# Router fed with centred rows, the last two tiles routed one by one in a written order, and gathered rows in other memory

## The chip, the cores and the metric

The kernel runs on one core of a Trainium2 chip. The number that counts is the device time of one execution in microseconds (us). The engines of the core are named as the profile names them: PE (TensorE, matrix products; PEld loads its weights), DVE (VectorE), ACT (ScalarE), POOL (GpSimd) and SP (SyncE, which here only issues DMAs).

## What the program computes

One hybrid decoder layer over 2048 tokens of width 1024, in float32. Only the end of the mixer, the router and the experts matter here:

```
mix = concatenate([y_conv, y_dn]) @ w_out
x   = layer_norm(ALPHA * x + gate1 * mix, ln1_g, ln1_b)
h   = x * (1 + scale2) + shift2
group   = top 1 of softmax(h @ w_grp + b_grp)                 # 4 groups
experts = top 2 of softmax((h @ w_exp + b_exp)[group])        # 8 experts in a group
y[token] += gate * ((silu(xb @ w_gate[e]) * (xb @ w_up[e])) @ w_down[e])   # for each chosen expert e
x = layer_norm(ALPHA * x + gate2 * y, ln2_g, ln2_b)
```

The tokens' rows h are regrouped by expert: each token has two entries (token, weight) in lists of the 32 experts, and an expert's rows are fetched by its list.

## The kernel before, in words

The program has a mixer stage and an expert stage. At the end of the mixer stage the 2048 tokens are 16 tiles of 128 rows (`mix_tile`, t = 0 to 15). For each tile PE makes two halves of `mix` (n = 0, 1), each of 24 products of 128x512: 8 slices k of the contraction, and for each slice three products, because both operands are split into a high and a low part (`y_hi`, `y_lo`, `wo_hi`, `wo_lo`). DVE adds the old x to each half and sums the row (L896), ACT squares and sums (L900), DVE finds the inverse deviation by three Newton steps on 128x1 numbers (`ln_root`, L918 to L924) and makes two normalised rows from x: `h` for the router and the experts (G2, B2) and `x_t` for the residual (Ga, Ba), two DVE instructions of 128x1024 each (L903, L904). SP stores both to DRAM (`d_h2`, `d_xa`).

Router work lags behind the tiles: `mix_tile` puts functions into the list `later`, and takes one out at fixed points (`slots`) of the following tiles. `logits` turns a tile's h by eight PE transposes into PSUM (`hT`), copies them by ACT (`hTs`) and multiplies by the router's weights (`lg`, 8 products that run as 16 passes of 128x40). `route` runs for a pair of tiles (t-1, t): DVE finds group, experts and weights (L951 to L991). `rank` finds each entry's place in the experts' lists (L999 to L1022; five small PE products count the tokens ahead), and POOL writes the entries into `d_list` with indirect DMAs, two for each tile (L1025). What is left in `later` after tile 15 (its logits, and route and rank of the pair 14, 15) is done by `flush`, behind the last product.

Meanwhile the weights of experts 0 and 1 (gate and up) are loaded while tiles are left to do (`load_first`), and `split_up(0)` makes a high part (ACT, `gu_hi`) and a low part (DVE, `gu_lo`) of those of expert 0.

The expert stage (`moe`) issues in this order on SP: down weights of expert 0 (`load_down(0)`), gate and up weights of expert 2 (`load_up(2)`), down weights of expert 1, and then the first six lists of each of two blocks (`entries`, tile `idx`), which wait until all entries have landed in `d_list`. POOL then gathers the rows of expert 0 and of expert 1 (`gather`, `hr<-d_h,idx`, 512 KB each), PE turns them (`pT`), ACT and DVE split them (`xT_hi`, `xT_lo`), and the first expert's products begin (`pg`). From then on PE goes through 32 experts.

In the mixer stage a scheduler of the framework sets the order on every engine, from the order in which the code issues and from estimated costs; inside `manual_schedule` (before: `moe` on all engines, `tail` on SP) the engines named keep the order of the code. Each engine runs its instructions strictly in order, and SP's DMA issues wait on SP for what they depend on. Tiles come from pools; a tile that reuses memory waits for what last used it.

Of the kernel before, what the change touches and what calls it, by code (L numbers as in the profile page):

```python
# [10 lines left out]
F32 = mybir.dt.float32  # L11
# [9 lines left out]
P = 128  # L21
D = 1024
# [31 lines left out]
class Layer:  # L54
# [774 lines left out]
    def router_consts(self):  # L829
# [10 lines left out]
        nc.gpsimd.iota(self.iota, pattern=[[1, 32]], base=0, channel_multiplier=0, allow_small_or_imprecise_dtypes=True)  # L840
        self.tok = c.tile([P, NT, 2], I32, name="tok")
# [32 lines left out]
    def mix_tile(self, t):  # L874
        nc = self.nc
        v = nc.vector
# [3 lines left out]
        sm = lambda n, w=1: self.small.tile([P, w], F32, tag="n_" + n, bufs=2, name=n)  # L880
        st, nm, ssq = sm("st", 2), sm("nm"), sm("ssq")

        slots = ((0, 7), (1, 3)) if t % 2 else ((1, 1), (1, 5))
        for n in range(2):
            ps = self.acc("mix")
            i = 0
            for k in range(KD):
                for a, b in ((hi, 0), (hi, 1), (lo, 0)):
                    nc.tensor.matmul(ps, a[:, k, :], self.wo[n][b][:, k, :], start=i == 0, stop=i == 3 * KD - 1)  # L889
                    i += 1  # L890
                if k % 2:
                    yield
                if (n, k) in (slots if t else ((0, 3), (0, 7), (1, 3))) and self.later:
                    self.later.pop(0)()
            xs = x[:, n * 512:(n + 1) * 512]
            v.scalar_tensor_tensor(xs, xs, ALPHA, ps, op0=OP.mult, op1=OP.add, accum_out=st[:, n:n + 1])  # L896

        h = self.t4(name="h2")
        v.tensor_scalar(nm, st[:, 0:1], st[:, 1:2], -1.0 / D, op0=OP.add, op1=OP.mult)
        nc.scalar.activation(h, x, AF.Square, bias=nm, accum_out=ssq)  # L900
# [12 lines left out]
    def ln_root(self, ssq, sm):  # L913

        v = self.nc.vector
        ve, hv, rs, t = sm("ve"), sm("hv"), sm("rs"), sm("t")
        i = self.small.tile([P, 1], I32, tag="n_i", bufs=2, name="rsi")
# [4 lines left out]
        for _ in range(3):  # L922
            v.scalar_tensor_tensor(t, rs, hv, rs, op0=OP.mult, op1=OP.mult)
            v.scalar_tensor_tensor(rs, t, 1.5, rs, op0=OP.add, op1=OP.mult)  # L924
        return rs


    def logits(self, t, h):
        nc = self.nc
# [8 lines left out]
        if t % 2 == 0:  # L938
            self.pl = self.prt.tile([P, 512], F32, tag="rt", name="lg")
        o = t % 2 * 40  # L940
        for k in range(KD):
            nc.tensor.matmul(self.pl[:, o:o + 40], hT[k // 4][:, (k % 4) * P:(k % 4 + 1) * P], self.wr[:, k, :], start=k == 0, stop=k == KD - 1)

    def route(self, t):
# [4 lines left out]
        sm = self.rs_ = lambda n, s, dt=F32: self.small.tile([P] + list(s), dt, tag="r_" + n, bufs=2 if n in ("ent", "pi", "ge", "d", "ew") else 1, name=n)  # L949
# [9 lines left out]
        ex, se = sm("ex", (4,)), sm("se", (2,))  # L959
        for j in range(2):  # L960
# [5 lines left out]
        v.tensor_tensor(oh, self.iota[:, None, 0:4].to_broadcast([P, 2, 4]), gi[:, :, None].to_broadcast([P, 2, 4]), op=OP.is_equal)  # L966
        t84 = sm("t84", (2, 8, 4))
        for j in range(2):
# [5 lines left out]
        for j in range(2):  # L974
# [8 lines left out]
        for j in range(2):  # L983
# [9 lines left out]
    def rank(self, t):  # L993
        nc = self.nc
        v = nc.vector
        pl, ent, sm = self.pl, self.ent, self.rs_
# [9 lines left out]
        pr = pl[:, 128:224]  # L1006
        mm = nc.tensor.matmul
        mm(pr[:, 0:32], self.Us, ob[:, 0], start=True, stop=True)
        mm(pr[:, 32:64], self.ob, ob[:, 0], start=True, stop=False)
        mm(pr[:, 32:64], self.Us, ob[:, 1], start=False, stop=True)  # L1010
        mm(pr[:, 64:96], self.ob, ob[:, 0], start=True, stop=False)
        mm(pr[:, 64:96], self.ob, ob[:, 1], start=False, stop=True)
        rk = sm("rk", (2, 32))
        v.tensor_tensor(rk, pr[:, 0:64].rearrange("p (j c) -> p j c", j=2), self.base[:, None, :].to_broadcast([P, 2, 32]), op=OP.add)
        v.tensor_tensor(self.base, self.base, pr[:, 64:96], op=OP.add)
        for j in range(2):
# [6 lines left out]
        for j in range(2):  # L1023
# [16 lines left out]
    def moe_pools(self, st):  # L1040
        p = lambda **k: self.pool(st, **k)
# [648 lines left out]
```

## Time and profile before

| | us |
|---|---|
| median of 3 runs (lowest, highest) | 1768.59 (1767.44, 1770.77) |
| the profiled execution | 1770.56 |
| its span, first to last instruction | 1768.9 |
| mean granted PE clock, share of full | 0.956 |

| stretch of the profiled execution, us | length | PE busy | granted clock | DMA share |
|---|---|---|---|---|
| 1100 to 1166, mixer's last tiles | 66 | 65.93 | 1.00 | 0.37 |
| 1166 to 1205, between last mix product and first expert product | 39 | 7.85 | 0.52 | 0.49 |
| 1300 to 1400, experts | 100 | 94.35 | 1.00 | 0.91 |

Busy is the time in which an engine executes; idle time of an engine costs only where others wait for it. The granted clock is the share of 2.4 GHz that PE was given: 1.00 is 2.4 GHz, 0.50 is 1.2 GHz. In a row of the timeline the numbers are start and duration, then engine, source line, operation, the tile written and those read, the shape, how many instructions were merged, and in brackets how long the engine was idle ahead of it and for whom.

### The profile page before, as it was taken

The page shows a single profiled execution, that of the slowest core. Times are in us where ns is not written, and L with a number is a line of the kernel's source. Part 1 is how long each engine was busy: PE and PEld are TensorE (multiplying, and loading weights), DVE is VectorE, ACT ScalarE, POOL GpSimd, SP SyncE. Part 2 cuts the span into 40 slices and gives each one's busy share as a digit, 9 for nine tenths or more (in the row PEclk, how much of TensorE's full clock was granted, in tenths as well). Part 3 has the DMA queues.
Part 4 walks back from the last instruction along what each step waited for, and adds up shares of the span by engine and source line. Part 5 has one row for each costly group of instructions (what it writes and reads, how often), then busy time and mean ns, then how long its engine had stood idle before and what let it go on. Part 6 is the DMA issues. An engine that isn't in the chain of part 4 may idle for free. (4 is left out here: it accounts for less than half of the span.)

```text
span 1768.9 us, 25248 instructions
## 1 busy us (share of the span) xinstructions
PE 1565.4 (88%) x7784; PEld 1261.1 (71%) x7784; DVE 1254.1 (71%) x3010; ACT 775.4 (44%) x1603; POOL 534.7 (30%) x441
## 2 busy tenths in 40 slices
PE   6899999998999999999889999957999989999800
PEld 4678877776777778888678888845777778778600
DVE  6777667766877987574688887665667686876554
ACT  4433455445233336344443322226545565554452
POOL 3200111021110003022320211215556675765517
PEclk9999999999999999999999999978999999999955
DMA  9553586455764758544477854347989998998464
GB/s 282 166 184 100 167 249 192 127 136 161 219 198 144 214 163 252 141 99 118 143 241 227 256 168 144 138 160 224 298 259 290 285 316 265 294 305 240 105 221 178
DMA packets 347943, 356.79 MB, mean 202 GB/s; under 512 B 49705, under 2 KB 283778, under 8 KB 347794
## 3 DMA queue, kind: packets, MB, share of 16 engines
q1 hardware_dynamic: 330546, 316.61, 56.4%
q0 software_dynamic: 17248, 38.37, 9.2%
q8 instruction: 71, 1.16, 0.3%
q14 instruction: 78, 0.64, 0.1%
HBM read 268.83 MB, written 101.79 MB: 210 GB/s over the span
## 5 line engine op out<-in xcount | busy, mean ns | idle before, releaser
L280 PE MATMUL acc<-hhi,w_hi 128*128 128x512 f32 x896 | 365.6, 409 | 7.4 <-ACT st L444 3.2
L280 PE MATMUL acc<-hlo,w_hi 128*128 128x512 f32 x896 | 360.6, 403 | 1.7 <-DVE hlo L337 1.0
L280 PE MATMUL acc<-hhi,w_lo 128*128 128x512 f32 x896 | 361.0, 403 | 0.0
L280 PEld LDWEIGHTS acc<-hhi,w_hi 128*128 128x128 f32 x896 | 171.3, 191 | 48.6 <-ACT st L444 4.1
L280 PEld LDWEIGHTS acc<-hlo,w_hi 128*128 128x128 f32 x896 | 170.7, 191 | 40.8 <-DVE hlo L337 2.4
L280 PEld LDWEIGHTS acc<-hhi,w_lo 128*128 128x128 f32 x896 | 170.9, 191 | 39.7 <-issue 1.7
L1093 DVE TENSOR_TENSOR gu_lo<-gu_raw,gu_hi 128x1024 fp32r<-128x1024 f32 (+1 forms) x132 | 179.7, 1404 | 24.1 <-ACT gu_hi L1092 15.7
L1102 POOL TENSOR_TENSOR dn<-dn_raw,dn 128x1024 fp32r<-128x1024 f32 x64 | 168.2, 2655 | 58.4 <-ACT dn L1101 56.1
L1135 PE MATMUL pg<-gu_hi,xT_hi 128*128 128x512 f32 x376 | 150.0, 399 | 1.2 <-ACT xT_hi L1125 1.2
L1135 PE MATMUL pg<-gu_hi,xT_lo 128*128 128x512 f32 x376 | 147.5, 392 | 0.1
L1135 PE MATMUL pg<-gu_lo,xT_hi 128*128 128x512 f32 x376 | 147.3, 392 | 0.0
L1092 ACT ACTIVATE gu_hi<-gu_raw 128x1024 fp32r<-128x1024 f32 (+1 forms) x132 | 129.0, 1035 | 4.6 <-PE mix L889 2.8
L1168 PE MATMUL pd<-dn,hT_hi 128*128 128x512 f32 x376 | 120.6, 402 | 6.2 <-PEq L1211 2.5
L453 DVE SCALAR_TENSOR_TENSOR cv<-st,cw,cv 128x512 f32<-128x512 f32 x144 | 108.5, 754 | 2.1
L1182 POOL DMA_INDIRECT d_xa<-y,idx x47 | 77.1, 1640 | 105.9 <-DVE y L1176 46.3
L889 PE MATMUL mix<-wo_hi,y_hi 128*128 128x512 f32 x256 | 105.1, 411 | 0.0
L889 PE MATMUL mix<-wo_hi,y_lo 128*128 128x512 f32 x256 | 103.6, 404 | 1.2 <-DVE y_lo L871 1.2
L889 PE MATMUL mix<-wo_lo,y_hi 128*128 128x512 f32 x256 | 103.5, 404 | 0.0
L347 ACT ACTIVATE w_hi<-raw 128x1024 fp32r<-128x1024 f32 x56 | 59.6, 1065 | 93.4 <-PE acc L280 75.5
L1126 DVE TENSOR_TENSOR xT_lo<-pT,xT_hi 128x512 fp32r<-128x512 f32 x94 | 60.6, 686 | 39.1 <-ACT xT_hi L1125 35.2
L575 POOL TENSOR_SCALAR_AFFINE_SELECT gam<-gam 128x512 f32<-128x512 f32 x16 | 11.2, 701 | 252.7 <-ACT gam L574 241.7
L1168 PEld LDWEIGHTS pd<-dn,hT_hi 128*128 128x128 f32 x376 | 67.1, 188 | 27.4 <-issue 7.0
(352 smaller groups left out, 3255.1 us busy)
## 6 DMA issues: line engine op xcount, KB each, us to landing
dn_raw<-in_w_down_dram SPq DMA_DIRECT2D x32, 1024.0 KB
gu_raw<-in_w_gate_dram SPq DMA_DIRECT2D x60, 512.0 KB
gu_raw<-in_w_up_dram SPq DMA_DIRECT2D x60, 512.0 KB
raw<-in_w_in_dram SPq DMA_DIRECT2D x56, 512.0 KB
ada_w<-in_w_ada_dram SPq DMA_DIRECT2D x96, 256.0 KB
qkvT<-cv SPq DMA_DIRECT2D x48, 256.0 KB
x_t<-in_x_dram SPq DMA_DIRECT2D x16, 512.0 KB
y_raw<-yT SPq DMA_DIRECT2D x16, 512.0 KB
```

The costliest lines, as they stand in the source:

```text
L280: self.nc.tensor.matmul(ps, a[:, k, :], b[q][:, k, :], start=k + n == 0, stop=k == KD - 1 and n == 2)
L347: nc.scalar.activation(hi, raw, AF.Copy)
L453: nc.vector.scalar_tensor_tensor(y, st[:, t:t + 512], self.cw4[:, j, t:t + 1], y, op0=OP.mult, op1=OP.add)
L575: nc.gpsimd.affine_select(gam, gam, pattern=[[0, H], [1, P]], compare_op=OP.is_ge, fill=0.0, base=0, channel_multiplier=-1)
L889: nc.tensor.matmul(ps, a[:, k, :], self.wo[n][b][:, k, :], start=i == 0, stop=i == 3 * KD - 1)
L1092: nc.scalar.activation(hi[:, c], r, AF.Copy)
L1093: i = nc.vector.tensor_tensor(lo[:, c], r, hi[:, c].bitcast(F32), op=OP.subtract)
L1102: nc.gpsimd.tensor_tensor(dn[:, 1, k], r[:, k], dn[:, 0, k].bitcast(F32), op=OP.subtract)
L1126: nc.vector.tensor_tensor(lo[:, c], pT[n], hi[:, c].bitcast(F32), op=OP.subtract)
L1135: self.nc.tensor.matmul(ps, a[:, k], b[:, k], start=n == 0, stop=n == 3 * KD - 1)
L1168: self.nc.tensor.matmul(ps[n], hT[a][:, k], dn[:, b, k, c], start=i == 0, stop=i == 5)
L1182: i = self.nc.gpsimd.indirect_dma_start(out=self.d_xa, out_offset=bass.IndirectOffsetOnAxis(ap=idx[:, 0:1], axis=0), in_=y, in_offset=None ...
```

## The change

Four things change together.

- **Centred rows.** The router's products take (x - mean) * G2, without the division by the deviation and without B2. Each tile's inverse deviation stays in a tile `roots`, and `route` multiplies the logits by it (one DVE instruction for each tile in place of one for the pair). The part of B2 is put through the same transposes and products once (`router_bias`, in tile 1) and added to the router's bias. The normalised h is finished after the logits (`finish`), the residual x by `finish_x`.
- **Tiles 14 and 15 are routed one by one**, each with its own route, rank and lists.
- **Tile 15 is issued in an order by hand** (`last_tile`) on PE, ACT, DVE and SP, with the split of expert 0's weights in it. The stores of `x_t` of tiles 14 and 15 come at its end.
- **In `moe`** the first lists are read before `load_up(2)` and `load_down(1)`, not after; the pool of the gathered rows (`hrp`) is made ahead of that of the raw weights, which gives both other addresses.

```diff
 def mix_tile(self, t):
-        slots = ((0, 7), (1, 3)) if t % 2 else ((1, 1), (1, 5))
+        slots = ((0, 7), (1, 3)) if t % 2 else ((1, 1), (1, 5)) if 0 < t < NT - 2 else ((0, 3), (0, 7), (1, 3))
...
-        rs = self.ln_root(ssq, sm)
-        for o, g, b in ((h, self.G2, self.B2), (x, self.Ga, self.Ba)):
-            v.scalar_tensor_tensor(o, x, nm, g, op0=OP.add, op1=OP.mult)
-            v.scalar_tensor_tensor(o, o, rs, b, op0=OP.mult, op1=OP.add)
-        nc.sync.dma_start(self.d_h2[t * P:(t + 1) * P, :], h)
-        nc.sync.dma_start(self.d_xa[t * P:(t + 1) * P, :], x)
-        self.later.append(lambda: self.logits(t, h))
+        self.center(t, x, lo, h)
+        self.ln_root(t)
+        if t == NT - 2:
+            self.last = x, h
+            return
+        self.finish_x(t, x)
+
+        def logits():
+            self.logits(t, h)
+            self.finish(t, h)
+        self.later.append(logits)
         if t % 2:
             self.later += [lambda: self.route(t - 1), lambda: self.rank(t - 1)]
         if t == 0:
-            self.later.insert(0, lambda: None)
+            self.later.insert(0, self.router_bias)
...
+    def center(self, t, x, lo, h, parts=1):
...
+        v.tensor_scalar(nm, st[:, 0:1], st[:, 1:2], -1.0 / D, op0=OP.add, op1=OP.mult)
+        nc.scalar.activation(lo.rearrange("p k c -> p (k c)"), x, AF.Square, bias=nm, accum_out=ssq)
+        for i in range(parts):
+            c = slice(i * D // parts, (i + 1) * D // parts)
+            v.scalar_tensor_tensor(h[:, c], x[:, c], nm, self.G2[:, c], op0=OP.add, op1=OP.mult)
...
+    def last_tile(self):
...
+        mix(0, 0, 1)
+        turned = self.products_turn(h0)
+        mix(0, 1, 6)
+        self.pl = self.prt.tile([P, 512], F32, tag="rt", name="lg")
+        self.products_sum(self.pl[:, 0:40], turned)
+        mix(0, 6, KD)
+        self.finish(t - 1, h0)
+        self.route(t - 1, 1)
+        self.rank_count(t - 1, 1)
+        self.mix_sum(t, 0, ps[0], x)
+        ps.append(self.acc("mix"))
+        mix(1, 0, 6)
+        self.rank_sums(1)
+        mix(1, 6, KD)
...
+        self.rank_place(t - 1, 1)
+        self.mix_sum(t, 1, ps[1], x)
+        h = self.t4(name="h2")
+        self.center(t, x, lo, h, 2)
+        turned = self.products_turn(h)
+        self.ln_root(t)
...
+        self.products_sum(self.pl[:, 0:40], turned)
+        self.route(t, 1)
+        self.rank_count(t, 1)
+        self.rank_sums(1)
+        self.rank_place(t, 1)
+        self.finish(t, h)
+        for k in range(0, KD, 2):
+            v.tensor_tensor(wlo[:, k:k + 2], raw[k // 2], whi[:, k:k + 2].bitcast(F32), op=OP.subtract)
+        self.finish_x(t - 1, x0)
+        self.finish_x(t, x)
+
+    def router_bias(self):
+
+        pl = self.prt.tile([P, 512], F32, tag="rt", name="lgb")
+        self.products_sum(pl[:, 0:40], self.products_turn(self.B2))
+        self.nc.vector.tensor_tensor(self.br, self.br, pl[:, 0:40], op=OP.add)
...
 def route(self, t, w=2):
-        v.tensor_tensor(lg, pl[:, 0:80].rearrange("p (j c) -> p j c", j=2), self.br[:, None, :].to_broadcast([P, 2, 40]), op=OP.add)
+        for j in range(w):
+            v.scalar_tensor_tensor(lg[:, j], pl[:, 40 * j:40 * j + 40], self.roots[:, t + j:t + j + 1], self.br, op0=OP.mult, op1=OP.add)
...
 def moe_pools(self, st):
+        self.hrp = p(name="hrp", bufs=2)
         self.rawp = p(name="raw8", bufs=6)
-        self.hrp = p(name="hrp", bufs=2)
...
         self.load_down(0)
+        for j in range(2):
+            entries(j, 0, 6, self.entries)
         self.load_up(2)
         self.load_down(1)
-        for j in range(2):
-            entries(j, 0, 6, self.entries)
...
+            if t < NT - 1:
+                yield from self.mix_tile(t)
...
+        with self.tc.manual_schedule(engines={E.PE, E.Activation, E.DVE, E.SP}):
+            self.last_tile()
```

What the order on the engines becomes is seen at three places. First SP, where the mixer stage ends; `d_h` and `d_xa` are the stores of h and of the residual rows, `dn_raw` and `gu_raw` loads of expert weights, `idx` the reading of the lists. Before:

```order
L905 DMA d_h_124<-h_11102 128x1024
L906 DMA d_xa<-x_t 128x1024
L1080 DMA dn_raw<-in_w_down_dram 128x2x1024
L1059 DMA gu_raw<-in_w_gate_dram 128x4x256
L1059 DMA gu_raw<-in_w_up_dram 128x4x256
L1059 DMA gu_raw<-in_w_gate_dram 128x4x256
L1059 DMA gu_raw<-in_w_up_dram 128x4x256
L1080 DMA dn_raw<-in_w_down_dram 128x2x1024
L1229 DMA idx_11296<-d_list 128x6x4
L1229 DMA idx_11297<-d_list 128x6x4
```

And now:

```order
L949 DMA d_h_124<-h_11022 128x1024
L949 DMA d_h_124<-h_11185 128x1024
L955 DMA d_xa<-x_t 128x1024 x2
L1181 DMA dn_raw<-in_w_down_dram 128x2x1024
L1330 DMA idx_11359<-d_list 128x6x4
L1330 DMA idx_11360<-d_list 128x6x4
L1160 DMA gu_raw<-in_w_gate_dram 128x4x256
L1160 DMA gu_raw<-in_w_up_dram 128x4x256
```

The reading of the lists moved ahead of five loads, and it stays behind both stores of x_t and behind the first load of down weights, `dn_raw`. The program's list of waits for that load names, before, the store of h of tile 15 but not the store of x_t of tile 15; now it names the store of x_t of tile 15 too (the memory of the load is then other memory).

Second DVE, from the places of the last tile's entries (`pi`) on. Before:

```order
L1022 CAST pi<-pos 128x4
L1201 CAST sets<-sets_f 1x2
L1093 TENSOR_TENSOR gu_lo<-gu_raw_10528,gu_hi 128x512
L1093 TENSOR_TENSOR gu_lo<-gu_raw_10531,gu_hi 128x512
L1093 TENSOR_TENSOR gu_lo<-gu_raw_10534,gu_hi 128x512
```

And now:

```order
L1123 CAST pi<-pos 128x2
L948 SCALAR_TENSOR_TENSOR h_11185<-h_11185,roots,rows 128x1024
L999 TENSOR_TENSOR gu_lo<-gu_raw_10541,gu_hi 128x1024 x4
L953 SCALAR_TENSOR_TENSOR x_t<-x_t,nm,rows 128x1024
L1302 CAST sets<-sets_f 1x2
L954 SCALAR_TENSOR_TENSOR x_t<-x_t,roots,rows 128x1024
L953 SCALAR_TENSOR_TENSOR x_t<-x_t,nm,rows 128x1024
L954 SCALAR_TENSOR_TENSOR x_t<-x_t,roots,rows 128x1024
L1194 TENSOR_TENSOR gu_lo<-gu_raw_10544,gu_hi 128x512
```

Nine DVE instructions of 128x1024 that stood ahead of `pi` (the finishing of h and x, the split of expert 0's weights) now stand behind it.

Third PE, where tile 14 ends and tile 15 begins (`mix<-wo_hi,y_hi` opens a slice). The last product of tile 14 is the one above the first slice of three. Now:

```order
L1109 MATMUL lg<-ob,onesb 128x32
L911 MATMUL mix<-wo_hi,y_lo 128x512
L911 MATMUL mix<-wo_hi,y_hi 128x512
L911 MATMUL mix<-wo_lo,y_hi 128x512
L911 MATMUL mix<-wo_hi,y_lo 128x512
L1022 MATMUL hT<-ident,h_11022 128x128 x8
L911 MATMUL mix<-wo_hi,y_hi 128x512
```

Before, the transposes of tile 14's rows stood in the second half of tile 15:

```order
L889 MATMUL mix<-wo_hi,y_hi 128x512
L934 MATMUL hT<-ident,h_10973 128x128 x8
L889 MATMUL mix<-wo_lo,y_hi 128x512
L942 MATMUL lg<-wr,hTs 128x40 x4
L889 MATMUL mix<-wo_hi,y_lo 128x512
L942 MATMUL lg<-wr,hTs 128x40 x4
L889 MATMUL mix<-wo_hi,y_hi 128x512
```

They moved from near the end of tile 15 to its fourth product.

## Rows read from the trace of the kernel before

**Rows 1.** Windows, PE: stretch, length, busy us (instructions), granted clock, DMA share, GB/s.

```profile
925.00:930.00 5.00, 5.00 (x30) 1.00 0.94 282
1152.00:1166.00 14.00, 13.98 (x77) 1.00 0.30 113
1166.00:1205.00 39.00, 7.85 (x38) 0.52 0.49 161
```

**Rows 2.** Waits of PE, 890 to 1205 us: total, times, longest.

```profile
PE pT L1116 <- DMA hr<-d_h,idx: 18.3, 1, 18.3
```

**Rows 3.** Timeline from the last mix product to the first expert product.

```profile
1166.86 1.22 DVE L1093 TENSOR_TENSOR gu_lo<-gu_raw,gu_hi 128x1024 fp32r<-128x1024 f32 x1
1168.00 0.21 DVE L899 TENSOR_SCALAR nm<-st 128x1 f32<-128x1 f32 x1
...
1172.10 0.15 DVE L921 TENSOR_SCALAR rs<-rsi 128x1 int32<-128x1 int32 x1
...
1173.62 1.28 DVE L904 SCALAR_TENSOR_TENSOR h<-h,rs,rows 128x1024 f32<-128x1024 f32 x1
...
1176.83 3.63 PE L942 MATMUL lg<-wr,hTs 128*128 128x40 f32 x16
...
1180.50 0.24 DVE L951 TENSOR_TENSOR lg<-lg,br 128x80 f32<-128x80 f32 x1 [4.39 <-PE lg L942]
...
1185.83 0.17 DVE L1022 CAST pi<-pos 128x4 int32<-128x4 f32 x1
...
1190.54 0.95 POOL L1025 DMA_INDIRECT d_list<-ent,pi  x1 [0.30 <-issue]
1194.29 0.95 SPq L1229 DMA_DIRECT2D idx<-d_list  x2
...
1198.02 1.08 POOL L1106 DMA_INDIRECT hr<-d_h,idx  x1 [6.53 <-DMA idx<-d_list]
...
1202.66 1.94 PE L1116 MATMUL pT<-ident,hr 128*128 128x128 f32 x8 [18.28 <-DMA hr<-d_h,idx]
...
1205.28 0.76 PE L1135 MATMUL pg<-gu_hi,xT_hi 128*128 128x512 f32 x1 [0.68 <-ACT xT_hi L1125]
```

**Rows 4.** Timeline of PE, the mix products around one tile's router work (1161 to 1166 us).

```profile
1161.71 0.40 PE L889 MATMUL mix<-wo_hi,y_hi 128*128 128x512 f32 x1
...
1162.74 0.48 PE L889 MATMUL mix<-wo_lo,y_hi 128*128 128x512 f32 x1
...
1164.15 0.48 PE L889 MATMUL mix<-wo_hi,y_lo 128*128 128x512 f32 x1
...
1165.27 0.48 PE L889 MATMUL mix<-wo_hi,y_hi 128*128 128x512 f32 x1
...
1165.82 0.40 PE L889 MATMUL mix<-wo_hi,y_lo 128*128 128x512 f32 x1
```

**Rows 5.** Timeline of DVE: sum of a half, then the mean.

```profile
1066.42 0.68 DVE L896 SCALAR_TENSOR_TENSOR x_t<-x_t,mix 128x512 f32<-128x512 f32 x1
...
1067.16 0.20 DVE L899 TENSOR_SCALAR nm<-st 128x1 f32<-128x1 f32 x1
```

**Rows 6.** Windows, PE: the clock falls and rises (columns as in rows 1).

```profile
898.00:898.50 0.50, 0.05 (x1) 1.00 1.29 377
901.00:902.00 1.00, 0.00 (x0) 0.78 0.01 4
1167.50:1168.00 0.50, 0.00 (x0) 0.79 0.06 4
1208.50:1209.00 0.50, 0.50 (x3) 0.75 0.83 290
```

**Rows 7.** Timeline of SP: a store of x_t, and the next load into its buffer.

```profile
1062.34 0.32 SPq L906 DMA_DIRECT2D d_xa<-x_t  x1
...
1065.09 0.33 SPq L867 DMA_DIRECT2D x_t<-in_x_dram  x1
```

**Rows 8.** Scatters of expert rows; then windows with loads, with a gather.

```profile
DMA to landing us min/median/max: 4.5/6.1/8.4
1180.50:1186.00 5.50, 0.29 (x5) 0.18 (x4) 5.03 (x40) 2.77 (x7) 0.00 (x0) 0.50 1.06 371
1198.02:1202.66 4.64, 0.00 (x1) 0.04 (x1) 3.75 (x7) 2.45 (x5) 2.51 (x2) 0.50 0.51 139
```

More of the change, by code (lines that the diff above doesn't have):

```diff
@@ L840, in router_consts @@
         nc.gpsimd.iota(self.iota, pattern=[[1, 32]], base=0, channel_multiplier=0, allow_small_or_imprecise_dtypes=True)
+        self.roots = c.tile([P, NT], F32, name="roots")
         self.tok = c.tile([P, NT, 2], I32, name="tok")
@@ new lines, in finish_x @@
+    def finish_x(self, t, x):
+        v = self.nc.vector
+        v.scalar_tensor_tensor(x, x, self.means[t], self.Ga, op0=OP.add, op1=OP.mult)
+        v.scalar_tensor_tensor(x, x, self.roots[:, t:t + 1], self.Ba, op0=OP.mult, op1=OP.add)
+        self.nc.sync.dma_start(self.d_xa[t * P:(t + 1) * P, :], x)
+    def last_tile(self):
+        nc, v, t = self.nc, self.nc.vector, NT - 1
+        hi, lo, x = self.ready.pop(t)
+        x0, h0 = self.last
+        assert not self.later
+        self.stats(t)
+        ps = [self.acc("mix")]
+        mix = lambda n, a, b: [self.mix_product(ps[n], hi, lo, n, k) for k in range(a, b)]
+        mix(0, 0, 1)
[12 more added lines that the diff above has]
+        mix(1, 6, KD)
+        whi, wlo = self.t16([P, KD, 512], F32R, name="gu_hi"), self.t16([P, KD, 512], F32R, name="gu_lo")
+        self.w_up[0] = whi, wlo
+        raw = self.raw_up.pop(0)
+        for k in range(0, KD, 2):
+            nc.scalar.activation(whi[:, k:k + 2], raw[k // 2], AF.Copy)
+        self.rank_place(t - 1, 1)
[4 more added lines that the diff above has]
+        self.ln_root(t)
+        self.pl = self.prt.tile([P, 512], F32, tag="rt", name="lg")
+        self.products_sum(self.pl[:, 0:40], turned)
[4 more added lines that the diff above has]
+        self.finish(t, h)
+        for k in range(0, KD, 2):
+            v.tensor_tensor(wlo[:, k:k + 2], raw[k // 2], whi[:, k:k + 2].bitcast(F32), op=OP.subtract)
+        self.finish_x(t - 1, x0)
+        self.finish_x(t, x)
@@ L937, in logits, with products_sum, route @@
             hT.append(s)
-        if t % 2 == 0:
-            self.pl = self.prt.tile([P, 512], F32, tag="rt", name="lg")
-        o = t % 2 * 40
+        return hT
+    def products_sum(self, out, hT):
         for k in range(KD):
-            nc.tensor.matmul(self.pl[:, o:o + 40], hT[k // 4][:, (k % 4) * P:(k % 4 + 1) * P], self.wr[:, k, :], start=k == 0, stop=k == KD - 1)
-    def route(self, t):
+            self.nc.tensor.matmul(out, hT[k // 4][:, (k % 4) * P:(k % 4 + 1) * P], self.wr[:, k, :], start=k == 0, stop=k == KD - 1)
+    def route(self, t, w=2):
         nc = self.nc
@@ L948, in route @@
         X = mybir.AxisListType.X
-        sm = self.rs_ = lambda n, s, dt=F32: self.small.tile([P] + list(s), dt, tag="r_" + n, bufs=2 if n in ("ent", "pi", "ge", "d", "ew") else 1, name=n)
+        tl = lambda n, s, dt=F32: self.small.tile([P] + list(s), dt, tag="r_" + n, bufs=2 if n in ("ent", "pi", "ge", "d", "ew") else 1, name=n)
+        sm = self.rs_ = lambda n, s, dt=F32: tl(n, (2,) + tuple(s[1:]), dt)[:, 0:w]
         lg = sm("lg", (2, 40))
-        v.tensor_tensor(lg, pl[:, 0:80].rearrange("p (j c) -> p j c", j=2), self.br[:, None, :].to_broadcast([P, 2, 40]), op=OP.add)
+        for j in range(w):
+            v.scalar_tensor_tensor(lg[:, j], pl[:, 40 * j:40 * j + 40], self.roots[:, t + j:t + j + 1], self.br, op0=OP.mult, op1=OP.add)
         m8, i8 = sm("m8", (2, 8)), sm("i8", (2, 8), U32)
-        for j in range(2):
+        for j in range(w):
             v.max(m8[:, j], lg[:, j, 0:8])
@@ L958, in route @@
         v.tensor_scalar(nm, m8[:, :, 0], -1.0, None, op0=OP.mult)
-        ex, se = sm("ex", (4,)), sm("se", (2,))
-        for j in range(2):
+        ex, se = tl("ex", (4,)), sm("se", (2,))
+        for j in range(w):
             nc.scalar.activation(ex, lg[:, j, 0:4], AF.Exp, bias=nm[:, j:j + 1], accum_out=se[:, j:j + 1])
@@ L973, in route @@
         self.j8 = j8
-        for j in range(2):
+        for j in range(w):
             v.max(e8[:, j], el[:, j])
@@ L982, in route @@
         ent = self.ent = sm("ent", (2, 2, 4), I32)
-        for j in range(2):
+        for j in range(w):
             nc.gpsimd.tensor_copy(ent[:, j, :, 0], self.tok[:, t + j, 0:1].to_broadcast([P, 2]))
@@ L1022, in rank @@
         self.chain.append(v.tensor_copy(pi, pos))
-        for j in range(2):
+        for j in range(w):
             for k in range(2):
@@ L1231, in moe @@
         self.load_down(0)
+        for j in range(2):
+            entries(j, 0, 6, self.entries)
         self.load_up(2)
         self.load_down(1)
-        for j in range(2):
-            entries(j, 0, 6, self.entries)
         at = lambda e, j: idx[j][:, e, :]
```

93 lines of the change are left out of this document (56 added, 37 removed).

## The prediction

> **What bounds the kernel now.** I read the windows first [rows 1]. In the last mixer tiles PE is busy 13.98 of 14 us, and in the stretch in which tile 1 lies 5.00 of 5.00: there the path is PE, and an added PE instruction costs its whole length. Between 1166 and 1205 us PE is busy 7.85 of 39 us at half clock; then the experts occupy it again. The list of waits names the end of that hole, 18.3 us for the gathered rows [rows 2]; what made them late stands in the timeline [rows 3]. It is one chain, and each link sits on another engine: the last mix result at 1166.22 (1165.82 + 0.40, rows 4), mean and deviation on DVE, finished h at 1173.62, router products at 1176.83, logits on DVE at 1180.50, places `pi` until 1186.00, four scatters by POOL (the last ends at 1191.49), lists read at 1194.29, gather at 1198.02, rows landed by 1202.66, first expert product at 1205.28. Every microsecond won or lost on this chain moves the experts by as much. I take the expert stage behind it as unchanged in length, since its PE work is the same; so the sum is the shift of the mark at 1205.28.
>
> **The change, part by part.**
>
> *Router bias in tile 1.* Eight transposes and 16 passes more on PE. One such set is read from where mix products are pushed apart [rows 4]: starts at 1161.71, 1162.74, 1164.15, 1165.27 are 1.03, 1.41 and 1.12 us apart instead of the usual 0.23 (so two products later the last one starts at 1165.82), together 2.87 us more. PE has no idle time there to hide it [rows 1]. Term **+2.9**; bounds 2.0 (if some of it fills a wait of PE for the mixer's other half) and 3.5. DVE's one more small instruction for each tile is hidden under PE.
>
> *Tiles 0 to 13 else.* Centring, roots and finishing are the same number of large DVE instructions as before; only their order changes, and PE hides DVE here. In tile 14 the router work of tile 13 is taken out after nine products instead of sixteen; the centred rows are ready about 2.6 us after tile 13's last product (sum and mean by rows 5, then 1.28 for the rows), nine products last 2.1. Term **+0.5**, bounds 0 and 1.
>
> *Tile 15, the transposes of tile 14.* By the order they now stand behind only three of its products, 0.7 us. The rows need: the sum of the second half, 0.74 us from its start to the mean [rows 5], three short instructions between them in the new order, about 0.5, then 1.28; with the start 0.25 after the last product, some 3.0 us. PE stands for the difference. Term **+2.4**, bounds 1.8 and 3.0.
>
> *The clock.* After the last product (end 1166.22) the granted clock fell to 1.2 GHz within 1167.50 to 1168.00, about 1.6 us later [rows 6]. Of two gaps of 1.9 us near 900 us the first kept the clock (1.00 at 898) and in the second it fell (0.78 at 901 to 902). A gap of 2.4 is longer than both. Recovery: work at half speed from 1205.28 until about 1208.75 [rows 3, 6], 3.5 us for 1.75 us of work. Term **+1.5**, bounds 0 and 1.8.
>
> *From the last mix result to `pi`.* Before: 1166.22 to 1186.00, 19.8 us. Now: mean 0.8 us after the result (no split stands between sum and mean; before it was 1168.00, behind one of 1.14), half a row set 0.7 each, so the first transposes begin 1.75 after the result and the second set at 2.35. ACT's square ends at 2.4, its two copies at 3.0 and 3.6; 16 passes of the router behind the first copy, 2.07 us at full clock (tile 14's: 1.18 and 0.89 by rows 4), end at about 5.1. The Newton steps (1172.10 to 1173.62, 1.5 us, from 2.5 on) are done by then: this is the real gain, since 2 large instructions and the steps leave the chain. From the logits to the end of `pi` it took 5.50 us [rows 3]. One tile instead of two saves about a dozen short instructions, but the weights' instructions now stand ahead of the ranking and wait for ACT's exponential; I leave 5.5. So `pi` ends 10.7 us after the result: **-9.1**. The gap ahead of the first transposes is again 1.75 us, at the edge of the clock's fall; if it falls the 16 passes take 3.63 as in rows 3, 1.6 more. Half of it, **+0.8**; bounds 0 and 2.
>
> *From `pi` to the gather.* Before: 1186.00 to 1198.02, 12.0 us, of which four scatters are 5.5, their landing 2.8 and reading the list 3.73 [rows 3]. Two scatters now end 3.0 after `pi` and land at 5.8. But SP cannot read the lists then: ahead of that instruction stand the two stores of x_t and the load of down weights, and the second store waits for nine DVE instructions behind `pi`: h 1.2, four splits at 1.14 (1166.86 to 1168.00), four steps of x at 1.2 to 1.28, together **10.9 us**. The load ahead of the lists waits for that store to land: 2.75 us from a store's issue to the load that reuses its buffer [rows 7]. Then 0.4 for the load's issue and 3.73 from the list's issue to the gather: 10.9 + 2.75 + 0.4 + 3.73 = 17.8. Term **+5.8**, bounds 4.8 and 7.5. Reading the lists ahead of five loads gives nothing, since these had been issued long before the list could be read.
>
> *Gather beside loads.* Before, the 4 MB of weights were through when the gather ran (139 GB/s in its 4.64 us). Now they are issued from about 14 us after `pi` on, and at 371 GB/s [rows 8] take 11 us: the gather falls into them. No row shows a gather beside these loads. Nearest is the scatter of expert rows, which lands in 4.5 to 8.4 us, median 6.1, in a stage full of loads [rows 8]: 1.6 over its least. Term **+1.5**; bounds 0 (own queue, no loss) and 6 (behind the 2.2 MB that are left then). The Trainium skill (DMA: Bandwidth & Descriptors, Queues, rings and completion order) says that a DMA engine takes turns between the queues that have work, packet by packet. By that rule the gather would get at least half of 371 GB/s, 2.8 us for 512 KB, and the term would be nearer 0.5 and the whole sum 5.3; no run here shows it yet.
>
> *The other memory.* The blanking of the gathered rows moves out of the chain, but ACT was not what the gather waited for (rows 2 and 3 name the list). Nothing.
>
> Sum: 2.9 + 0.5 + 2.4 + 1.5 - 9.1 + 0.8 + 5.8 + 1.5 = **+6.3 us**. The profiled execution took 1770.56 (span 1768.9), 2.0 over the median, within the runs' spread; I set the shift on the median: 1768.59 + 6.3 = **1774.9**.
>
> **Rivals.** 0.2%, 3.5 us, is about what a measurement of this kernel can tell from no change.
>
> A, the clock stays up and the gather is not slowed: both gaps are of the size at which it held once. 6.3 - 1.5 - 0.8 - 1.5 = +2.5, 1771.1, no change. For it: the first gap near 900 us; against it, the second and the fall at 1167.8.
>
> B, the gather queues behind the loads: +6 instead of +1.5, so +10.8, 1779.4. For it: DMA share 1.06 with loads alone [rows 8], nothing left over. Against it: the gather comes from POOL, another queue than SP's.
>
> C, the other side: SP is not held. If the stores of x_t were issued before the lists land (5.8 us after `pi`), the lists would be read then, 8.3 us sooner: 6.3 - 8.3 = -2.0, 1766.6, no change; with the clock up as well -4.3, 1764.3, faster. It decides where DVE has x of tile 15 ready: below 3 us behind `pi` the gain stands. Against it: nine large instructions stand there in order, and DVE runs in order.
>
> **Chances.** Forecast (+3.5 to +9.5) 0.50, A 0.25, B 0.12, C 0.13, of which 0.08 is below -3.5. Faster 0.08, same 0.30 (A and the rest of C), slower 0.62. The range from 1768.5 (about A with its bounds) to 1780.5 (B and the upper bounds) leaves out most of C and the far end of B, some 2 in 10; the forecast's own range is 1772 to 1778.
>
> **What would show it.** In the changed profile: eight transposes of the bias row in tile 1; PE idle some 2.4 us for DVE ahead of tile 14's transposes, with the clock at 0.50 behind it; `pi` some 11 us after the last mix result; the list's reading some 14 us after `pi`, just behind the second store of x_t; the gather landing later than 4.64 us; the first expert product some 6 us later than at 1205.28, and from there on the same length to the end. I am wrong if the lists are read within 8 us of `pi`, or if the experts' first blocks wait for weights that now come later: gate and up weights of expert 2 are issued only then, and I take them as in time.

## The result and the profile after

The changed kernel takes **1785.03 us** (median of 4 runs, 1784.10 to 1785.39), the kernel before 1768.69 on the same chip. The ratio is **1.009**, 95% interval 1.0073 to 1.0108: slower by some 16 us. Timed once more (e12) it stood at 1.0093 (1.0069 to 1.0117). The sign was forecast, the size (+6.3 us) was not, and the range ended at 1780.5.

First the stretch that answers to [rows 3]: lines of the timeline of the changed kernel from tile 14's transposes to the first expert product.

```profile
1156.77 1.09 PE L1022 MATMUL hT<-ident,h 128*128 128x128 f32 x8 [1.97 <-DVE h L930]
...
1171.87 0.69 DVE L919 SCALAR_TENSOR_TENSOR x_t<-x_t,mix 128x512 f32<-128x512 f32 x1 [0.29 <-PE mix L911]
...
1173.75 1.23 PE L1022 MATMUL hT<-ident,h 128*128 128x128 f32 x8 [1.92 <-DVE h L930]
...
1184.24 0.17 DVE L1123 CAST pi<-pos 128x2 int32<-128x2 f32 x1
1184.31 1.28 DVE L948 SCALAR_TENSOR_TENSOR h<-h,roots,rows 128x1024 f32<-128x1024 f32 x1
...
1185.51 4.62 DVE L999 TENSOR_TENSOR gu_lo<-gu_raw,gu_hi 128x1024 fp32r<-128x1024 f32 x4
...
1186.73 1.97 POOL L1126 DMA_INDIRECT d_list<-ent,pi  x1 [0.30 <-issue]
...
1192.68 2.84 SPq L955 DMA_DIRECT2D d_xa<-x_t  x2
1193.88 1.28 DVE L954 SCALAR_TENSOR_TENSOR x_t<-x_t,roots,rows 128x1024 f32<-128x1024 f32 x1
...
1197.94 0.38 SPq L1181 DMA_DIRECT2D dn_raw<-in_w_down_dram  x1
...
1198.68 0.96 SPq L1330 DMA_DIRECT2D idx<-d_list  x2
1199.68 0.67 SPq L1160 DMA_DIRECT2D gu_raw<-in_w_gate_dram  x1
...
1203.89 0.51 SPq L1181 DMA_DIRECT2D dn_raw<-in_w_down_dram  x1
1205.06 1.06 POOL L1207 DMA_INDIRECT hr<-d_h,idx  x1 [16.37 <-DMA gu_raw<-in_w_gate_dram]
...
1213.78 1.94 PE L1217 MATMUL pT<-ident,hr 128*128 128x128 f32 x8 [30.62 <-DMA hr<-d_h,idx]
...
1216.77 0.77 PE L1236 MATMUL pg<-gu_hi,xT_hi 128*128 128x512 f32 x1 [1.04 <-ACT xT_hi L1226]
```

Read it as one chain again. The last mix result comes at 1171.83 instead of 1166.22: +5.6. The places end at 1184.41, 12.6 us behind it instead of 19.8: -7.2. The lists are read at 1198.68, 14.3 us behind the places instead of 8.3: +6.0. The gather follows 6.4 us later instead of 3.7: +2.65. The rows are there after 8.7 us instead of 4.6: +4.1. The first expert product follows 3.0 us later instead of 2.6. Together +11.5: it stands at 1216.77 instead of 1205.28.

Windows of the changed kernel, columns as in [rows 1], with busy us (instructions) of PE, its weight loads, DVE, ACT and POOL in turn: tile 15, the reading of the lists, the gather, the first expert products.

```profile
1158.00:1161.00 3.00, 3.00 (x9) 2.33 (x8) 1.82 (x4) 0.54 (x2) 2.56 (x2) 0.50 0.06 20
1198.70:1205.00 6.30, 0.00 (x0) 0.00 (x0) 4.16 (x7) 2.86 (x6) 0.00 (x0) 0.50 0.96 272
1205.00:1213.80 8.80, 0.02 (x1) 0.05 (x1) 0.00 (x0) 0.00 (x0) 2.08 (x2) 0.50 1.05 367
1217.00:1222.40 5.40, 5.40 (x13) 4.21 (x14) 0.08 (x1) 2.34 (x2) 3.35 (x2) 0.50 0.62 112
```

In this execution PE works at half clock in part of tile 15, and again from the first expert product until about 1222.8 (before: 1208.75). The second block's first product stands at 1227.27 instead of 1214.55, so the +11.5 have become +12.7, and they stay so to the end of the experts; the span is 13.5 longer. The medians lie 16.3 apart, since the profiled execution of before was 1.9 above its median and that of the changed kernel 0.9 below.

### The profile page after: what moved, and what is told of

The parts are those of the page before. It is cut to its first block, busy times and chain, and to the rows that moved or that the text cites. A ratio compares the mean times of both kernels' runs of the same rounds, so it can differ in the third digit from the quotient of the medians.

```text
span 1782.4 us, 25343 instructions
## 1 busy us (share of the span) xinstructions
PE 1569.6 (88%) x7807; PEld 1263.9 (71%) x7807; DVE 1257.2 (71%) x3037; ACT 776.0 (44%) x1606; POOL 540.4 (30%) x442
## 5 line engine op out<-in xcount | busy, mean ns | idle before, releaser
L1194 DVE TENSOR_TENSOR gu_lo<-gu_raw,gu_hi 128x1024 fp32r<-128x1024 f32 (+1 forms) x128 | 172.3, 1389 | 16.3 <-ACT gu_hi L1193 10.6
L1193 ACT ACTIVATE gu_hi<-gu_raw 128x1024 fp32r<-128x1024 f32 (+1 forms) x128 | 125.1, 1035 | 1.9
L1227 DVE TENSOR_TENSOR xT_lo<-pT,xT_hi 128x512 fp32r<-128x512 f32 x94 | 60.6, 686 | 48.7 <-ACT xT_hi L1226 45.8
L1126 POOL DMA_INDIRECT d_list<-ent,pi x32 | 38.0, 1186 | 161.3 <-DVE pi L1123 99.4
```

The costliest lines, as they stand in the source:

```text
L1126: i = nc.gpsimd.indirect_dma_start(out=self.d_list, out_offset=bass.IndirectOffsetOnAxis(ap=pi[:, j, k:k + 1], axis=0), in_=ent[:, j, k, : ...
L1193: nc.scalar.activation(hi[:, c], r, AF.Copy)
L1194: i = nc.vector.tensor_tensor(lo[:, c], r, hi[:, c].bitcast(F32), op=OP.subtract)
L1227: nc.vector.tensor_tensor(lo[:, c], pT[n], hi[:, c].bitcast(F32), op=OP.subtract)
```

## The experiments

**Theory.** SP, held by the stores of x_t, lets the weights go so late that they meet the reading of the lists and the gather. **Rivals:** the lists wait for something else than SP; the rows come late for a reason of their own (other memory); the order of loads and lists does nothing. In the table the places are the end of `pi`, the reading is the issue of `idx`, the gather is its issue, the rows are there when PE begins to turn them, and the first product is `pg`. e6, which computes something else, is left out. The stretches in us, from the timelines of single executions (before and changed kernel first), with the ratio to the kernel before:

| run | last result to places | to reading | to gather | to rows | to first product | sum | ratio (95%) |
|---|---|---|---|---|---|---|---|
| before | 19.8 | 8.3 | 3.7 | 4.6 | 2.6 | 39.1 | 1 |
| changed | 12.6 | 14.3 | 6.4 | 8.7 | 3.0 | 44.9 | 1.0090 (1.0073-1.0108) |
| e1 | 12.7 | 6.4 | 5.1 | 9.2 | 3.0 | 36.4 | 1.0043 (1.0023-1.0063) |
| e2 | 12.6 | 6.5 | 4.6 | 4.8 | 3.0 | 31.4 | 1.0017 (0.9998-1.0036) |
| e3 | 13.0 | 14.3 | 6.1 | 4.6 | 3.0 | 41.0 | 1.0073 (1.0036-1.0109) |
| e4 | 13.0 | 11.5 | 3.4 | 7.4 | 3.0 | 38.3 | 1.0060 (1.0036-1.0084) |
| e5 | 12.0 | 14.3 | 6.3 | 8.5 | 3.0 | 44.1 | 1.0073 (1.0052-1.0094) |
| e7 | 15.9 | 10.3 | 3.6 | 4.6 | 2.6 | 37.0 | 1.0007 (0.9989-1.0026) |
| e8 | 19.8 | 6.8 | 3.8 | 8.0 | 3.0 | 41.3 | 1.0013 (0.9994-1.0032) |
| e9 | 12.6 | 5.6 | 3.3 | 4.8 | 3.0 | 29.2 | 0.9991 (0.9973-1.0010) |
| e10 | 12.4 | 5.6 | 3.3 | 4.9 | 2.4 | 28.6 | 0.9993 (0.9976-1.0010) |
| e11 | 12.5 | 5.6 | 3.3 | 4.7 | 2.4 | 28.5 | 0.9992 (0.9974-1.0011) |
| e12 | 12.9 | 14.3 | 6.2 | 9.5 | 3.0 | 45.8 | 1.0093 (1.0069-1.0117) |

**e1: x_t early.** In `last_tile`:

```diff
         self.products_sum(self.pl[:, 0:40], turned)
+        self.finish_x(t - 1, x0)
         mix(0, 6, KD)
...
         self.ln_root(t)
+        self.finish_x(t, x)
...
-        self.finish_x(t - 1, x0)
-        self.finish_x(t, x)
```

> The changed kernel with the four DVE steps of x_t (and so the two stores) moved ahead of the router's work: those of tile 14 ahead of its h, those of tile 15 behind its Newton steps. Theory (SP is held by these stores, 14.3 us from pi to the lists' reading): the lists are read as soon as the scatters have landed, about 7 us behind pi, so 7 us sooner, but the loads behind the lists still meet the gather (8.7 us from gather to rows): 1785.0 - 7 = 1778, between 1775 and 1780. Rival (the lists wait for something else than the stores, such as the store of h or the scatters): the reading stays 14 us behind pi and the time stays at 1785.

The timeline of e1, the last scatter, SP and the gather:

```profile
1188.04 1.97 POOL L1126 DMA_INDIRECT d_list<-ent,pi  x1 [0.30 <-issue]
...
1189.71 0.38 SPq L1181 DMA_DIRECT2D dn_raw<-in_w_down_dram  x1
...
1192.12 0.96 SPq L1330 DMA_DIRECT2D idx<-d_list  x2
...
1197.19 1.54 POOL L1207 DMA_INDIRECT hr<-d_h,idx  x1 [7.18 <-DVE gu_lo L1194]
...
1206.40 1.94 PE L1217 MATMUL pT<-ident,hr 128*128 128x128 f32 x8 [21.92 <-DMA hr<-d_h,idx]
```

The reading came 6.4 us behind the places (1185.72), 2.1 behind the last scatter's end, and the time went down by half of what had been lost. SP's hold is shown: what the lists waited for were those stores. The gather took 9.2 us, as slow as in the changed kernel.

**e2: as e1, and the 3 MB behind the first gathers.**

```diff
-        self.load_up(2)
-        self.load_down(1)
...
         first = [fetch(e, 0) for e in range(2)]
+        self.load_up(2, first)      # its first load waits for both gathers
+        self.load_down(1)
```

> As the run before it, and the gate/up weights of expert 2 and the down weights of expert 1 are loaded only behind the first two gathers. Theory (these 3 MB, let loose together with the lists, slow their reading by 2.65 us and the gather by 4.1 us): idx to gather 3.7 to 4.5 us, gather to rows 4.6 us, so 5 to 7 us less than the run before it: 1771, between 1769 and 1775. Rival (the rows come late for a reason of their own, such as other memory or a colder queue): the same time as the run before it.

The gather is back at 4.8 us, and the two edits together take back some four fifths of the loss: 1.0017. The timeline of e2, SP and the first gather:

```profile
1193.28 0.38 SPq L1183 DMA_DIRECT2D dn_raw<-in_w_down_dram  x1
...
1195.76 0.96 SPq L1332 DMA_DIRECT2D idx<-d_list  x2
...
1200.36 1.41 POOL L1209 DMA_INDIRECT hr<-d_h,idx  x1 [6.78 <-DVE gu_lo L1196]
...
1205.13 1.94 PE L1219 MATMUL pT<-ident,hr 128*128 128x128 f32 x8 [17.08 <-DMA hr<-d_h,idx]
```

**e3 and e4: which load slows what.** e3 is the changed kernel with the edit of e2 alone; e4 is the changed kernel with

```diff
-        self.load_down(0)
         for j in range(2):
             entries(j, 0, 6, self.entries)
+        self.load_down(0)
         self.load_up(2)
```

> The changed kernel with these 3 MB loaded behind the first two gathers and nothing else moved; SP is held as before and the 1 MB of down weights of expert 0 still stand ahead of the lists. Theory of contention: gather to rows back to 4.6 us (-4.1) at 1781; if the loads behind the lists also slowed their reading, idx to gather 3.7 (-2.65) and 1778; if the 1 MB ahead of the lists did it, idx to gather stays 6.4. Rival (no contention, or what is saved comes back as a wait for the later weights): 1785.

> The changed kernel with the down weights of expert 0 loaded behind the lists instead of ahead of them. The lists no longer wait for that load, which waits for the second store of x_t to land: reading 3 us sooner, at 11 us behind pi. If the 1 MB ahead of the lists slowed their reading (6.4 us from idx to gather), that comes back to 3.7 and the time is 1785.0 - 3.2 - 2.65 = 1779; if the 3 MB behind them did, 4 MB behind them slow it as much or more: 1782 or above. Gather to rows 8.7 us or longer in both.

They answer crosswise. Without the 3 MB behind the lists (e3) the gather is back at 4.6, but from reading to gather it still takes 6.1. Without the 1 MB ahead of them (e4) that falls to 3.4, with 4 MB behind them, and the gather takes 7.4. So the 1 MB queued ahead on SP slows the lists, and the loads behind them slow the gather. The timeline of e4 shows the loads beside the gather, and no `dn_raw` ahead of `idx`:

```profile
1204.72 1.08 SPq L1330 DMA_DIRECT2D idx<-d_list  x2
...
1206.85 0.37 SPq L1181 DMA_DIRECT2D dn_raw<-in_w_down_dram  x1
...
1208.14 1.44 POOL L1207 DMA_INDIRECT hr<-d_h,idx  x1 [10.65 <-DVE gu_lo L1194]
...
1210.00 3.85 SPq L1181 DMA_DIRECT2D dn_raw<-in_w_down_dram  x1
```

**e5: tile 14's transposes later.**

```diff
-        mix(0, 0, 1)
+        mix(0, 0, 3)
         turned = self.products_turn(h0)
-        mix(0, 1, 6)
+        mix(0, 3, 6)
```

> The changed kernel with tile 14's transposes behind nine products of tile 15 instead of three. Theory (the path is PE there): PE's wait of 1.97 us for the centred rows falls below 0.7, the clock stays up (the ten products behind it at 0.23 us instead of 0.43, 1.7 us), tile 14's places are written as early as before, and the last mix result comes 3 to 3.7 us sooner; everything behind it moves along: ratio 1.007, some 3 us under the changed kernel. Rival (DVE or ACT then come late with tile 14's routing and hold the last sum): the last mix result moves by less than 1 us.

PE's wait fell from 1.97 to 0.57 us and the clock stayed up. From the last sum of tile 14 to that of tile 15 it took 14.8 us instead of 17.7 (14.1 before): 2.9 gained, just under what I expected, and 1.0073 for the whole. But only 1.4 of it can be put down to the shorter wait: in e12, the changed kernel again, and in e1, e2 and e6 the clock stayed at 1.00 behind the full wait, and tile 15 took 16.2 us there. That the edit keeps the clock up is not shown. The line of PE's timeline in e5, then the same line and a window behind it in e12:

```profile
1168.62 1.09 PE L1022 MATMUL hT<-ident,h 128*128 128x128 f32 x8 [0.57 <-DVE h L930]
...
1155.66 1.09 PE L1022 MATMUL hT<-ident,h 128*128 128x128 f32 x8 [1.98 <-DVE h L930]
...
1157.02:1159.02 2.00, 2.00 (x10) 1.58 (x9) 1.73 (x4) 0.42 (x1) 1.70 (x2) 1.00 0.02 1
```

**e6: no bias row.**

```diff
-            self.later.insert(0, self.router_bias)
+            self.later.insert(0, lambda: None)
```

> The changed kernel without the router products of the bias row (the logits lack that part). Theory: PE loses 8 transposes and 16 passes on its path, the stretch from the first product of tile 1 to the first of tile 15 is 2 to 2.9 us shorter, ratio 1.0075. Rival (they lie in waits of PE): that stretch the same within 0.5 us, ratio 1.009.

The second half of tile 1 takes 10.5 us, and 13.1 in the changed kernel: 2.6 for the bias row. The stretch that I had named, from the first product of tile 1 to that of tile 15, took 235.7 us and 238.1 in the changed kernel: 2.4, as expected. In the other runs with the bias row and the same order of these tiles it took 237.8 to 240.5, so this price is known to some 2 us only. The whole run took 1845.1 us (ratio 1.0411), and my 1.0075 for it was a miss; with other logits other tokens go to the experts, so its time is no price of the bias row.

**e7: centred rows alone.** The last two tiles go through `mix_tile` like the others, `split_up(0)` and `flush` as before, loads and pools of `moe` as before:

```diff
-            if t < NT - 1:
-                yield from self.mix_tile(t)
+            yield from self.mix_tile(t)
...
-            self.last_tile()
+        for _ in self.split_up(0):
+            pass
+        self.flush()
```

> Centred rows alone: the last two tiles go the way of the others, loads, lists and memory of the expert stage as in the kernel before. Theory (centring gains by itself, what loses is the order by hand behind it): first product of the router's tail 6 us sooner after the last mix result, places some 13 us after it instead of 19.8, four scatters and the lists as before (8 us from places to reading, 3.7 to the gather, 4.6 to the rows); with 2.3 us for the bias row the experts begin 4 to 5 us sooner than before: ratio 0.9975 (0.996 to 0.999). Rival (the stores of x and h or the split weights come between here too): reading 10 us or more behind the places, ratio 1.000 or above.

No difference: the rival was nearer. Of the 6.8 us that I expected between result and places 3.9 came, since two DVE steps of x_t and h lie between the logits of the two tiles. The loads start 13.5 us behind the last result instead of 11.5, so they still run when the four scatters do, and the lists are read 4.8 us behind the last scatter's end instead of 2.8 [rows 3]. The stretch is 2.1 us shorter, and the bias row takes 2.6.

**e8: the order and the memory of `moe` alone**, on the kernel before.

> The kernel before with only the order of the loads and lists and the place of the gathered rows of the changed one. Theory of contention: the 3 MB that were loaded during the routing now start with the lists' reading and meet the gather: idx to gather 3.7 us as before (the 1 MB ahead of the lists is long through), gather to rows 8.7 to 9.2 instead of 4.6: ratio 1.0025, 4 to 4.5 us slower. Rival, as I had it in the prediction (the order alone does nothing): ratio 1.000.

Its timeline, the last scatter, SP and the gather:

```profile
1191.38 0.97 POOL L1025 DMA_INDIRECT d_list<-ent,pi  x1 [0.30 <-issue]
...
1193.59 0.96 SPq L1229 DMA_DIRECT2D idx<-d_list  x2
...
1194.59 0.54 SPq L1059 DMA_DIRECT2D gu_raw<-in_w_gate_dram  x1
...
1196.82 0.67 SPq L1080 DMA_DIRECT2D dn_raw<-in_w_down_dram  x1
...
1197.37 1.05 POOL L1106 DMA_INDIRECT hr<-d_h,idx  x1 [5.01 <-ACT gu_hi L1092]
...
1205.37 1.94 PE L1116 MATMUL pT<-ident,hr 128*128 128x128 f32 x8 [20.03 <-DMA hr<-d_h,idx]
```

The gather took 8.0 us instead of 4.6 without anything of the mixer changed. Against that the lists were read 1.2 us behind the last scatter's end (1192.35 to 1193.59) instead of 2.8 [rows 3], since no loads ran beside the scatters. Net +2.3 us in the stretches; the ratio's interval still holds 1.

**e9: what was found, together**: e1, e5, and all three loads behind the first gathers.

> The changed kernel with the causes found so far taken out together: x_t and its stores early, all 4 MB of the next weights behind the first two gathers, tile 14's transposes behind nine products. Theory, from the stretches of the runs so far: last mix result to places 12.0, places to reading 6.4, reading to gather 3.5, gather to rows 4.7, rows to first product 3.0, together 29.6 us against 39.1 of the kernel before; on the other side 2.6 for the bias row, 0.7 for the wait in tile 15, up to 2 in tile 0 and 1 for the clock behind the first products: 3 to 5 us faster than before, ratio 0.9975. Rival (the down weights of expert 0 then come too late for its second half, and what is saved is waited for there): ratio 1.000.

The stretch came out at 29.2 us, as forecast, 9.8 less than before, but the time is level with the kernel before. In its trace the experts begin only 2.2 us earlier than before, since the last mix result comes 7.6 later. Of these 5.1 are there at tile 0's first product already (897.74 instead of 892.67 us), ahead of all that the change touches; 2.5 arise in tiles 0 to 15, with the bias row. From expert 2 on the experts run 0.4 earlier: PE waits there for DVE, 0.6 and 1.1 us, behind the splits of expert 2's weights, which come later than before. Between 1671 us and the last product another 2.0 are lost, where the clock falls (0.80 from 1675 to 1680 us). Counted from tile 0's first product the execution is 2.0 us shorter than that of before. The ratio's interval (0.9973 to 1.0010) holds that, and no change as well.

**e10: PE kept at work; e11: hidden rows first.** e10 adds to e9:

```diff
+            for _ in range(fill * (1 - n)):        # products_turn(h, 12)
+                nc.tensor.transpose(ps[:, 0:P], self.ident, self.ident)
...
+        for _ in range(102):
+            nc.tensor.transpose(self.pTs[0][:, 0], self.ident, self.ident)
         turn(0, 0)
```

> As the run before it, with PE kept at work where it waits: 12 transposes of the identity ahead of tile 15's transposes and 102 ahead of the first expert's, whose results nothing reads. Theory (the waits cost a second time through the clock): the 16 passes of the router in 1.9 us instead of 3.6 and the first products at 0.23 us instead of 0.43 from the start, 3 to 4.5 us less than the run before it, ratio 0.9955. Rival (the fillers end too late or the clock falls all the same): ratio as the run before it, or above.

The clock did what it should: the router's passes took 1.98 us instead of 3.47, the first expert products stood 0.23 apart from the start. Still no gain. The places came only 0.2 us sooner, since DVE now had the steps of x_t ahead of the logits; and in expert 0 the won time was given back, as the list of waits of that stretch says (1199 to 1215 us; total, times, longest):

```profile
ACT dn L1206 <- DMA dn_raw<-in_w_down_dram: 7.2, 1, 7.2
...
PE ph L1257 <- DVE hid L1248: 3.4, 1, 3.4
```

e11 adds, to take that wait away:

```diff
-                next(sd)
+                if e:
+                    next(sd)
                 act(e, 0)
+                if not e:
+                    next(sd)
                 next(sd)
```

> As the run with PE kept at work, but in expert 0 ACT's activation of the hidden rows stands ahead of the two halves of its down weights. There ACT waited 7.2 us for those weights, since they were held behind the gathers, and PE waited 3.4 us for the hidden rows behind it. Theory (what the early rows and the clock had won was given back at this wait): PE's wait there falls below 1 us and the experts run 2.5 to 3.5 us sooner than in that run, ratio 0.9975. Rival (the next late load takes its place, the gate and up weights of expert 2 or the down weights themselves): ratio 0.999 to 1.000 again.

The wait fell to 0.7 us and the experts ran 3.0 to 3.4 us ahead of the kernel before as far as 1648 us. The ratio is 0.9992 all the same. In the one profile the lead is gone at the end: between there and the last product 1.9 of it are lost, where the clock falls, and 1.4 more from the last product to the last stage's first load. e9's profile loses 2.0 of it too, e10's 0.4; what decides that stays open. So does the clock at the first products: in e11 the added transposes ended 1.2 us ahead of the gathered rows instead of 0.2 in e10, and the products ran 0.43 us apart until 1203.3.

**e12: the changed kernel again.**

> The changed kernel itself once more, on the chip and in the rounds of these runs. Ratio 1.009 (1.0073 to 1.0108), and in its profile the stretches as before: 14.3 us from places to reading, 6.4 to the gather, 8.7 to the rows. The first half of tile 0 took 12.6 us in the first profile of it and 16.0 to 16.9 in those of its variants; if 12.6 was the odd one, it is 16 or above here and that explains why the medians stood 3 us further apart than the profiled executions; if it is 12.6 again, something else does.

The same ratio and the same stretches. The first half of tile 0 took 13.7 us, so that explanation of the medians falls. The span was 1780.0, 11.1 over that of before, but this execution was the fastest of its six, and in it tile 0's first product came 2.8 us sooner than in the profile of before (889.85 instead of 892.67 us; 892.66 in the first profile of the changed kernel). Counted from that product the two profiles of the changed kernel are 13.5 and 14.0 us longer than that of before. Both lie within the interval of the ratio, 12.9 to 19.1 us, so the 16.3 between the medians leave nothing that needs a cause of its own.

## Why the prediction was wrong

*Router bias, +2.9:* right; 2.4 and 2.6 by e6. *Tiles 0 to 13 else, +0.5:* not to be told from the spread of tile 0, whose first half took 12.6 to 16.9 us in the executions shown here.

*Wait for tile 14's transposes, +2.4, and the clock behind it, +1.5:* right in kind and nearly in size, 1.97 (the first line above) and 1.5 (nine steps between products from 1157.93 to 1161.57, 3.64 us instead of 2.1). But the second belongs to the execution and not to the kernel: e12 waited 1.98 us and kept its clock, as e1, e2 and e6 did; e3 and e4 lost it. So one half of rival A's first condition can hold (in the tail the clock fell each time), and that this term came out so near is luck in part. Up to the last mix result the sum said +7.3, and the trace +5.6.

*Last result to places, -9.1 and +0.8:* -7.2. The clock fell in the tail for all of the 16 passes (3.64 us), so +1.6 belonged there instead of the half that I took.

*Places to reading:* 14.05 us expected, 14.27 measured. DVE's nine instructions end at 1195.16, 10.75 behind the places (10.9 expected). e1 shows that this is SP's hold. Rival C, SP not held, is out for the change as made; e1 shows what it would have given: 7.9 us sooner, but not its time, since the loads still met the gather.

*Reading to gather, 3.73 kept from before:* **the first step that failed.** I had seen the load ahead of the lists only as something that SP waits for. Its 1 MB also runs ahead of them: 6.4 us, and 3.4 without it (e4). In the traces' packets the lists begin to move 3.5 us behind their issue with the load 0.7 us ahead (e3 too), and 1.0 us with none near (before, e9).

*Gather beside loads, +1.5:* **the second, and the larger.** It was +4.1, and e2, e3 and e8 show the loads as the cause: 4.6 to 4.8 without them, 7.4 to 9.5 with them. I had priced it by the scatters among the experts [rows 8] and chosen near the lower end. All DMA moved 367 GB/s while the gather ran, as much as loads alone [rows 8], but the 512 KB took 8.7 us to land. Of the 4.1 some 2.9 lie ahead of the rows' first packet. By the trace's DMA packets it moved 4.7 us behind the gather's issue, in the other runs with loads beside it (e1, e4, e5, e8, e12) after 4.7 to 5.1, and without them after 1.8 to 2.1 (before, e2, e3, e7, e9 to e11). The DMA queues of the changed kernel (q0 has the gathers, q1 what SP issues; packets, MB, share of 16 engines), from 1205.06 to 1209.70 us and from 1209.75 to 1213.78:

```profile
q1 hardware_dynamic: 1445, 1.54, 106.2%
...
q1 hardware_dynamic: 241, 0.86, 53.8%
q0 software_dynamic: 223, 0.78, 48.9%
```

Why the first packet comes so late beside loads stays open. The rule of the Trainium skill (DMA: Bandwidth & Descriptors, Queues, rings and completion order), turns between queues, spoke for less still, +0.5. The second window, 0.78 against 0.86 MB, agrees with turns; the first, in which no row moved, is what I had left out when I made +0.5 of it. The same section of the Trainium skill says that each DMA engine consumes the descriptors of one queue in ring order; lists that wait behind the 1 MB on SP's queue, and not for the loads behind them, agree with it (e3, e4). Rival B had the sum of both effects nearly right, +6 against 2.65 + 4.1 = 6.8, but put all of it on the gather: the rows did not wait for the end of the loads, and the lists lost too.

*Expert stage unchanged:* nearly. The weights of expert 2 were in time, but PE needed 6.1 us at the first products until its clock rose (3.5 before): another 1.3. This too varies by execution: in e12 it was 4.0 us, and 0.4 were lost.

*The order does nothing, the other memory nothing:* e8 shows +3.4 in the gather and -1.5 ahead of it. The new memory of the rows does not slow them: e2, e3 and e9 have it too, and the gather took 4.6 to 4.8 us. That `dn_raw` lies on x_t's addresses is part of the hold, and e4 put a price of 2.8 us on it: reading 11.5 us behind the places instead of 14.3.

So +5.6 - 7.2 + 6.0 + 2.65 + 4.1 + 0.4 + 1.3 = 12.8 where I had 6.3. The two failed steps are 2.65 + 2.6 = 5.3 of the difference of 6.5; in the rest -1.7 ahead of the last result stands against +1.1 in the tail, +1.3 at the first products and 0.6 in small parts. The two steps stand in each profile that has the loads where the change put them (e5 and e12: 6.3 and 6.2 us to the gather, 8.5 and 9.5 to the rows).

## What to carry over

A load that is hidden in a gap of the chain has a place in time, not only in a queue: whoever shortens or holds that gap must ask what it meets next. Price every small transfer of the chain, lists and gathers, with the bulk loads beside it and ahead of it in its queue, and take the pessimistic bound when the volume left (here 4 MB, 11 us) is longer than the stretch it falls into. And a store at the end of an engine's work, on a queue that also carries the next stage's first read, sits on the critical path though nobody waits for its data. Last, a stretch of one execution is no price where the clock decides: the same wait in tile 15 cost 1.5 us more in one execution of the changed kernel than in the other.

## What the runs showed of the hardware

- From the issue of a gather of 128 rows of 4 KB to the work on its rows it took 4.6 to 4.9 us with no loads beside it and 8.0 to 9.5 us beside 3 MB from SP's queue (e4, beside 4 MB: 7.4). Its first packet moved 1.8 to 2.1 us behind the issue without loads, and 4.7 to 5.1 us with them.
- Two reads of 12 KB of lists behind a 1 MB load on the same queue let the gather go 6.0 to 6.4 us after their issue when it was issued 0.7 us ahead, 4.6 to 5.1 when 2.4 us ahead, and 3.3 to 3.8 with no load just ahead.
- Scatters of 16-byte entries let the next read go 1.2 to 1.3 us behind their end with no loads beside them (e8, e9), 2.1 with 1 MB (e1), 2.8 and 4.8 us with 4 MB (before, e7).
- Behind a wait of 1.97 to 1.98 us in tile 15 PE's granted clock fell to 0.50 in three executions (the changed kernel, e3, e4) and stayed at 1.00 in four (e1, e2, e6 and e12, the changed kernel again). Behind the 1.92 us ahead of the tail's transposes it was at 0.50 over the 16 passes in eight executions and at 0.60 in e5. Behind 0.57 us it stayed up (e5).
- Transposes of the identity in PE's waits kept the clock at 1.00 in the tail of e10 and e11. Ahead of the first expert's products they did so in e10, where they ended 0.2 us ahead of the gathered rows, and not in e11, where they ended 1.2 us ahead.
